# Mixer A of an fp32-split network: TensorE's instructions kept in the order of the text, side work two steps later in the local group, and short chains a step ahead of their transposes

## The chip, the core and the metric

The kernel runs on one core of a Trainium2 chip, whose engines are TensorE (PE in the views, with its weight loads as PEld), VectorE (DVE), ScalarE (ACT), GpSimd (POOL) and SyncE (SP, which issues most transfers). The metric is the device time of one execution in microseconds (us).

## What is computed

A network on 512 tokens of width 1024. Its first half-layer, mixer A, is a dilated attention with three head groups per head: group 0 is local, groups 1 and 2 see keys at strides 4 and 16. The three groups' outputs are mixed by a softmax over their log-sum-exps. Behind mixer A come a feed-forward layer, mixer B (latent attention), and further layers, which the change does not touch.

```python
DIL_CONFIGS = ((128, 1), (512, 4), (2048, 16))   # 8 heads of 128
...
    qkv = (h @ w_qkv).reshape(B, S, 3, N_GROUPS, A_HEADS, A_HEAD_DIM)
    outs, lses = [], []
    for g, (window, dil) in enumerate(DIL_CONFIGS):
        q = rope(rms_norm(qkv[:, :, 0, g], q_gain[g]), S)
        k = rope(rms_norm(qkv[:, :, 1, g], k_gain[g]), S)
        v = qkv[:, :, 2, g]
        o, lse = dilated_group(q, k, v, window, dil)
        outs.append(o)
        lses.append(lse)
    wts = jax.nn.softmax(jnp.stack(lses, 0), axis=0)
    o = wts[0][..., None] * outs[0]
    for g in range(1, N_GROUPS):
        o = o + wts[g][..., None] * outs[g]
    return o.reshape(B, S, A_WIDTH).astype(h.dtype) @ w_o
```

## The kernel before

Every fp32 product is made of three matmuls of split operands (a high and a low part, lines L144 to L146 in `mm3`). A weight tile arrives as `w_raw`, ScalarE copies its high part (`w_hi`, L129) and VectorE its low part (`w_lo`, L130).

Mixer A goes through four quarters `qd` of two heads each, and in each quarter through the groups g = 1, 2, 0. The projection of a group is the main work: groups 1 and 2 take 128x256 or 128x512 products of strided tokens four blocks b at a time, followed by `rotate_pair` for each block; group 0 (`project`) takes q, k and v in turn (`wh` 0 to 2) with `rotate` behind q and k. A rotate is a short serial chain over four engines: ScalarE squares (L419, tile `t`), GpSimd takes powers (L200, L201), ScalarE scales k (`yk`, L426), VectorE multiplies by the tables (L434, L435) and adds (L436). Its scratch tile `t2` exists once, so rotates follow one another. The result `t` is transposed by TensorE (`turn`, L443) and copied out by ScalarE (`qT`, `kT`, L445).

The attention of the group before is the side work. It is a generator that gives up control at each `yield`, and it is stepped once at each `yield` of the projection (12 matmuls in g = 0). `attend_strided` has two turns, two softmax steps, two `flip`s (transposes of the probabilities, L556, with a copy `pt`, L558) and two `values` (L567). `attend_local` turns kT, has four softmax steps (scores L535, mask L543, maximum L545, bias L546, exponentials L549), and then the combine chain that mixes the groups: L614 to L616 on VectorE, an exponential on ScalarE (L617), L618 to L623 on VectorE, which gives the weights `ce`. They are transposed on TensorE (L625, below "the transpose of ce"), copied to `crow` (L627), written to memory and read back as `f` (two transfers one after the other). The probabilities of group 0 are weighted with `ce` (L642), flipped and multiplied with v, and `og` is summed (L648, L649) and split into `oh` and `ol` (L162, L163). A third generator, `post`, is `out_pair`: the output projection of the quarter before (8 steps of 6 matmuls). After the last quarter only the attention of its group 0 is left, with `out_pair` of quarter 2 woven in, and then `out_pair` of quarter 3.

In what order each engine executes all this is not the order of the text: a scheduler reorders the instructions of all engines by its own model of their times. One block of code elsewhere (`Ahead`, a small class) calls a list of functions one ahead: it runs the first when it is made, and at each call returns the result that it holds and runs the next function.

Of the kernel before, what the change touches and what calls it, by code (L numbers as in the profile page):

```python
# [9 lines left out]
F32 = mybir.dt.float32  # L10
# [9 lines left out]
S = 512  # L20
# [36 lines left out]
def drain(gen):  # L57
    for _ in gen:
        pass
# [27 lines left out]
class Net:  # L87
# [253 lines left out]
    def mixer_a(self, pool):  # L341
# [126 lines left out]
        def project_strided(qd, g, u, vs):  # L468

            c0 = g * D + qd * 256  # L470
            wt = wide(c0, 3 * D + c0, nc.gpsimd if (qd, g) == (0, 1) else None)
            tab = tables(qd, g)
            u["rq"] = pool.tile([P, 8], F32, name="rq", tag="rq", bufs=3)
            pre = []
            for bp in range(2):
                for banks in both(wt, bp):
                    if banks:
                        pre += [rotate_pair(u, 2 * bp + i, ps, tab) for i, ps in enumerate(banks)]
                    yield
            u["pre"] = lambda wh: lambda b, h: pre[b][:, (2 * wh + h) * P:(2 * wh + h + 1) * P]  # L480
            if g == 1:
                wt = wide(7 * D + qd * 256, 8 * D + qd * 256)
                v12 = pool.tile([P, NB, 512], F32, name="v12", tag="v12", bufs=1)
                for bp in range(2):
                    for banks in both(wt, bp):
                        for i, ps in enumerate(banks or ()):
                            nc.scalar.copy(out=v12[:, 2 * bp + i, :], in_=ps)  # L487
                        yield
                vs[1], vs[2] = v12[:, :, 0:256], v12[:, :, 256:512]
            u["v"] = vs[g]  # L490
# [62 lines left out]
        def flip(pr):  # L553
            t = self.tbank()
            for n in range(4):
                nc.tensor.transpose(t[:, n * P:(n + 1) * P], pr[:, n * P:(n + 1) * P], self.ident)  # L556
            pt = pool.tile([P, 512], F32, name="pt", tag="pt", bufs=2)
            nc.scalar.copy(out=pt, in_=t)  # L558
            return pt
# [12 lines left out]
        def attend_strided(qd, g, u, og):  # L572

            for wh, n in enumerate("qk"):
                turn(u, n + "T", u["pre"](wh))
                yield
            st = pool.tile([P, 2, 2, NB], F32, name="st", tag="st", bufs=3)
            prs = []
            for h in range(2):
                prs.append(softmax(u, g, h, 0, st))  # L580
                yield
            nc.sync.dma_start(out=st_dram[qd, g - 1].rearrange("n (p b) -> p n b", b=NB),
                              in_=st.rearrange("p s h b -> p (s h) b"))
            pts = []
            for h in range(2):
                pts.append(flip(prs[h]))
                yield
            for h in range(2):
                pv = values(u, g, h, [pts[h]])
                o = pool.tile([P, S], F32, name="og", tag="og", bufs=4)  # L590
                nc.scalar.copy(out=o.rearrange("p (m r) -> p r m", r=4), in_=pv.rearrange("p (r m) -> p r m", r=4))
                og[g, h] = o
                yield

        def attend_local(qd, u, og):

            turn(u, "kT", u["pre"](1))
            s = pool.tile([P, 2, 2, 8], F32, name="cs", tag="cs", bufs=1)
            nc.sync.dma_start(out=s.rearrange("p g s n -> p (g s n)"),
                              in_=st_dram[qd].rearrange("g n (b p) -> p (g n b)", p=P))  # L600
            yield
            st = pool.tile([P, 2, 2, NB], F32, name="st", tag="st", bufs=3)
            prs = []
            for h in range(2):
                for s0 in (0, 2):
                    prs.append(softmax(u, 0, h, s0, st))
                    yield

            own = st.rearrange("p s h b -> p s (h b)")
            T = lambda n, name: pool.tile([P, n, 8], F32, name=name, tag=name, bufs=1)  # L610
            lo, e, dn = T(1, "clo"), T(3, "ce"), T(3, "cd")
            tt = nc.vector.tensor_tensor
            tt(out=lo[:, 0], in0=s[:, 0, 0], in1=s[:, 1, 0], op=ALU.min)
            tt(out=lo[:, 0], in0=lo[:, 0], in1=own[:, 0], op=ALU.min)  # L614
            tt(out=e[:, 0:2], in0=lo.to_broadcast([P, 2, 8]), in1=s[:, :, 0], op=ALU.subtract)
            tt(out=e[:, 2], in0=lo[:, 0], in1=own[:, 0], op=ALU.subtract)  # L616
            nc.scalar.activation(out=e, in_=e, func=AF.Exp)  # L617
            tt(out=dn[:, 0:2], in0=e[:, 0:2], in1=s[:, :, 1], op=ALU.mult)  # L618
            tt(out=dn[:, 2], in0=e[:, 2], in1=own[:, 1], op=ALU.mult)
            tt(out=lo[:, 0], in0=dn[:, 0], in1=dn[:, 1], op=ALU.add)  # L620
            tt(out=lo[:, 0], in0=lo[:, 0], in1=dn[:, 2], op=ALU.add)
            nc.vector.reciprocal(out=lo, in_=lo)
            tt(out=e, in0=e, in1=lo.to_broadcast([P, 3, 8]), op=ALU.mult)  # L623
            t = self.tbank()
            nc.tensor.transpose(t[0:16, 0:P], e[:, 0:2].rearrange("p g n -> p (g n)"), self.ident)  # L625
            row = pool.tile([16, P], F32, name="crow", tag="crow", bufs=1)
            nc.scalar.copy(out=row, in_=t[0:16, 0:P])  # L627
            nc.sync.dma_start(out=f_dram[qd].rearrange("n b p -> (n b) p"), in_=row)
            fs = {}
            for h in range(2):  # L630
                for g in (1, 2):
                    f = pool.tile([P, S], F32, name="f", tag="f", bufs=3)
                    nc.sync.dma_start(out=f, in_=f_dram[qd, (g - 1) * 2 + h].rearrange("b p -> (b p)").partition_broadcast(P))
                    fs[g, h] = f
            yield
            for h in range(2):
                pts = []
                for n in range(2):
                    pr = prs[2 * h + n]
                    for i in range(2):  # L640
                        b = 2 * n + i
                        nc.vector.tensor_scalar(out=pr[:, i * 256:(i + 1) * 256], in0=pr[:, i * 256:(i + 1) * 256],  # L642
                                                scalar1=e[:, 2, h * NB + b:h * NB + b + 1], scalar2=None, op0=ALU.mult)
                    pts.append(flip(pr))
                    yield
                pv = values(u, 0, h, pts)
                for g in (1, 2):
                    tt(out=og[g, h], in0=og[g, h], in1=fs[g, h], op=ALU.mult)  # L648
                    tt(out=og[g, h], in0=og[1, h] if g == 2 else pv, in1=og[g, h], op=ALU.add)  # L649
                oh = pool.tile([P, S], F32R, name="oh", tag="oh", bufs=2)  # L650
                ol = pool.tile([P, S], F32R, name="ol", tag="ol", bufs=2)
                self.split(oh, ol, og[2, h])
                u["o", h] = (oh, ol)
                yield

        side, post = iter(()), iter(())
        for qd in range(4):
            og, vs = {}, {}
            for g in (1, 2, 0):
                u = {"qT": [None, None], "kT": [None, None]}  # L660
                for _ in project_strided(qd, g, u, vs) if g else project(qd, u):
                    next(post, None)
                    next(side, None)
                if g == 1 and qd == 0:
                    nc.sync.dma_start(out=masks, in_=a["k_masks"])

                    for t in (self.hTh, self.hTl):
                        nc.scalar.copy(out=t[:, :, S:S + 64], in_=t[:, :, 0:64].bitcast(F32))
                drain(side)
                drain(post)  # L670
                if g:
                    side = attend_strided(qd, g, u, og)
                else:
                    side = attend_local(qd, u, og)
                if g == 1 and qd in (1, 2):
                    post = self.out_pair(wo, qd - 1, last)
                if g == 0 and qd == 3:
                    post = self.out_pair(wo, 2, last)
                if g == 0:
                    last = u  # L680
        for n in range(11):
            next(side)
            if n > 1:
                next(post, None)
        drain(post)
        drain(side)
        drain(self.out_pair(wo, 3, last))

    def out_pair(self, wo, pr, u):
# [863 lines left out]
```

## Time and profile before

| what | value |
|---|---|
| median of 3 runs | 2560.22 us (2559.7 to 2561.13) |
| the profiled execution's own time | 2559.68 us |
| its span, first to last instruction | 2557.9 us |
| TensorE busy | 2439.0 us (95%) in 13988 matmuls |
| VectorE, ScalarE, GpSimd busy | 1664.4, 1177.3, 269.1 us |
| mean granted TensorE clock | 0.983 |

The span is what the trace covers; the profiled execution took 1.8 us more than that, and was half a microsecond faster than the median. Busy is the time in which an engine had an instruction of its own in work. The granted clock is the share of full speed at which TensorE ran: 1.00 is 2.4 GHz and 0.50 is 1.2 GHz. Mixer A reaches from about 10 to 622 us.

### The profile page before, as it was taken

How to read it: one execution, taken by the hardware profiler on the slowest of the kernel's cores; microseconds unless marked ns; L12 is line 12 of the kernel's file. 1: busy time of each engine (PE TensorE's matmuls, PEld its weight loads, DVE VectorE, ACT ScalarE, POOL GpSimd, SP SyncE). 2: the span in 40 equal slices, each digit the busy share in tenths (PEclk: the TensorE clock that was granted, in tenths of full speed). 3: DMA queues.
4: the chain of work that ended last, by engine and by line, in shares of the span. 5: the costliest groups of instructions: out<-in, count | busy, mean ns of one | idle time of the engine just before them, and what ended most of it. 6: DMA issues, size and time to landing. Idle time of an engine off the chain costs nothing.

```text
span 2557.9 us, 36467 instructions
## 1 busy us (share of the span) xinstructions
PE 2439.0 (95%) x13988; PEld 2159.6 (84%) x13988; DVE 1664.4 (65%) x2718; ACT 1177.3 (46%) x2562; POOL 269.1 (11%) x415
## 2 busy tenths in 40 slices
PE   7999999998999999999999999899998998799998
PEld 7999998997888887677888888899987876799997
DVE  4454454547767645787776646877758775877774
ACT  4554545464332324654332334544445774454442
POOL 5311111120000002320000000000012211100001
PEclk9999999999999999899999999999999999899999
DMA  7342333323555422111564432233332121143332
GB/s 235 117 115 86 101 105 112 112 68 102 191 168 159 141 80 94 33 58 34 182 199 150 148 99 91 92 107 99 100 116 87 55 74 50 50 124 99 100 99 83
DMA packets 230415, 275.97 MB, mean 108 GB/s; under 512 B 43120, under 2 KB 172336, under 8 KB 230240
## 3 DMA queue, kind: packets, MB, share of 16 engines
q1 hardware_dynamic: 229280, 270.49, 34.2%
q0 software_dynamic: 960, 3.15, 0.3%
q8 instruction: 110, 1.80, 0.3%
q14 instruction: 65, 0.53, 0.1%
HBM read 268.21 MB, written 5.38 MB: 107 GB/s over the span
## 4 chain that ended last, share of the span: by engine, by line
PE 74%; DVE 8%; issue 6%; ACT 5%; POOL 4%; DMA 2%; SPq 0%; POOLq 0%; DVEq 0%; ACTq 0%
PE ps_mm L144 21%; PE ps_mm L146 20%; PE ps_mm L145 20%; PE ps_at L144 2%; PE ps_at L145 2%; PE ps_at L146 2%; DMA w_raw<-ffn_w_in 1%; PE ps_tr L443 1%; PE ps_at L567 1%; PE ps_at L535 1%; POOL rk L201 1%; DVE w_lo L130 1%; POOL rq L201 1%; ACT w_hi L129 1%; POOL ss L200 1%
## 5 line engine op out<-in xcount | busy, mean ns | idle before, releaser
L130 DVE TENSOR_TENSOR w_lo<-w_raw,w_hi 128x1024 fp32r<-128x1024 f32 (+2 forms) x304 | 367.8, 1217 | 159.2 <-ACT w_hi L129 157.4
L129 ACT CAST w_hi<-w_raw 128x1024 fp32r<-128x1024 f32 (+2 forms) x308 | 317.0, 1040 | 242.8 <-PE ps_mm L146 165.4
L144 PE MATMUL ps_mm<-w_lo,hTh 128*128 128x256 f32 (+3 forms) x1100 | 390.1, 355 | 4.4 <-DVE t L435 3.5
L145 PE MATMUL ps_mm<-w_hi,hTl 128*128 128x256 f32 (+3 forms) x1100 | 373.3, 339 | 0.9 <-DVE hTl L163 0.9
L146 PE MATMUL ps_mm<-w_hi,hTh 128*128 128x256 f32 (+3 forms) x1100 | 371.8, 338 | 0.0
L144 PE MATMUL ps_mm<-hTl,w_hi 128*128 128x256 f32 (+1 forms) x960 | 324.2, 338 | 5.3 <-DVE hTl L163 4.4
L146 PE MATMUL ps_mm<-hTh,w_hi 128*128 128x256 f32 (+1 forms) x960 | 323.7, 337 | 0.0
L145 PE MATMUL ps_mm<-hTh,w_lo 128*128 128x256 f32 (+1 forms) x960 | 323.7, 337 | 0.0
L144 PEld LDWEIGHTS ps_mm<-w_lo,hTh 128*128 128x128 f32 x1100 | 257.5, 234 | 12.3 <-ACT v L487 3.8
L145 PEld LDWEIGHTS ps_mm<-w_hi,hTl 128*128 128x128 f32 x1100 | 258.4, 235 | 5.9 <-DVE hTl L163 1.5
L146 PEld LDWEIGHTS ps_mm<-w_hi,hTh 128*128 128x128 f32 x1100 | 257.2, 234 | 4.2 <-issue 0.6
L308 DVE TENSOR_TENSOR x_sb<-ps_mm,x_sb 128x512 f32<-128x512 f32 x176 | 120.6, 687 | 130.5 <-PE ps_mm L146 129.8
L144 PEld LDWEIGHTS ps_mm<-hTl,w_hi 128*128 128x128 f32 x960 | 182.2, 190 | 26.2 <-DVE hTl L163 5.1
L146 PE MATMUL ps_mm<-w_hi,ah 128*128 128x512 f32 x512 | 199.7, 390 | 0.0
L144 PE MATMUL ps_mm<-w_lo,ah 128*128 128x512 f32 x512 | 199.6, 390 | 0.0
L145 PE MATMUL ps_mm<-w_hi,al 128*128 128x512 f32 x512 | 199.5, 390 | 0.0
L145 PEld LDWEIGHTS ps_mm<-hTh,w_lo 128*128 128x128 f32 x960 | 182.4, 190 | 19.4
L146 PEld LDWEIGHTS ps_mm<-hTh,w_hi 128*128 128x128 f32 x960 | 182.2, 190 | 18.6
L162 ACT CAST w_hi<-w_raw 128x512 fp32r<-128x512 f32 x160 | 92.4, 619 | 119.0 <-PE ps_mm L146 86.5
L145 PE MATMUL ps_mm<-th,w_lo 128*128 128x256 f32 x480 | 135.8, 283 | 5.8 <-ACT zh L162 5.8
L144 PE MATMUL ps_mm<-tl,w_hi 128*128 128x256 f32 x480 | 137.1, 286 | 1.1 <-DVE pu L1046 0.6
L146 PE MATMUL ps_mm<-w_hi,gh 128*128 128x512 f32 x352 | 137.5, 390 | 0.0
(404 smaller groups left out, 5260.1 us busy)
## 6 DMA issues: line engine op xcount, KB each, us to landing
w_raw<-ffn_w SPq DMA_DIRECT2D x128, 512.0 KB
w_raw<-ffn_w_in SPq DMA_DIRECT2D x88, 512.0 KB
ada_w<-w_ada SPq DMA_DIRECT2D x72, 512.0 KB
w_raw<-a_w_qkv SPq DMA_DIRECT2D x96, 256.0 KB
w_raw<-ffn_w_out SPq DMA_DIRECT2D x44, 512.0 KB
w_raw<-a_w_qkv SPq DMA_DIRECT2D x24, 512.0 KB
w_raw<-w_mix_in SPq DMA_DIRECT2D x20, 512.0 KB
tab<-tab_a SPq DMA_DIRECT2D x36, 256.0 KB
```

The lines of the kernel that those rows point to most:

```text
L129: nc.scalar.copy(out=hi[:, :sz], in_=raw[:, :sz])
L130: (eng or nc.vector).tensor_tensor(out=lo[:, :sz], in0=raw[:, :sz], in1=hi[:, :sz].bitcast(F32), op=ALU.subtract)
L144: mm(ps, lh, rl, start=start, stop=False, skip_group_check=open_)
L145: mm(ps, ll, rh, start=False, stop=False, skip_group_check=open_)
L146: mm(ps, lh, rh, start=False, stop=stop, skip_group_check=open_)
L162: self.nc.scalar.copy(out=hi, in_=src)
L200: self.nc.gpsimd.tensor_scalar(out=ms, in0=ms, scalar1=eps, scalar2=None, op0=ALU.add)
L201: self.nc.gpsimd.tensor_tensor(out=out, in0=ms, in1=self.mhalf[:, :n], op=ALU.pow)
L308: self.nc.vector.tensor_tensor(out=xs, in0=ps, in1=xs, op=ALU.add)
L443: nc.tensor.transpose(t[:, b * P:(b + 1) * P], pick(b, h), self.ident)
L535: nc.tensor.matmul(sc[:, i * kpb * P:(i + 1) * kpb * P], lhs, kT[:, k0:k0 + kpb * P], start=True, stop=True)
L567: nc.tensor.matmul(pv[:, b * P:(b + 1) * P], u["v"][:, (b if g else (b - 1 + i) % NB), h * P:(h + 1) * P], pts[n // 4][:, (n % 4) * P:(n % ...
```

## The change

It has five parts, all in mixer A; no arithmetic is added, removed or resized.

- The whole loop over the quarters stands inside `manual_schedule(engines={PE})`: TensorE's instructions stay in the order of the text. The other engines' order is still the scheduler's.
- In the projection of group 0, the side work (attention of group 2) starts two yields later.
- A `yield` stands between the combine chain and the transpose of `ce` (L636 after).
- The weighting (L642, now `weigh`, L630) is called through `Ahead`, one step ahead of its flip.
- In the tail, `post` is stepped only beside six of the side steps, no longer from the third on beside each.

```diff
             tt(out=e, in0=e, in1=lo.to_broadcast([P, 3, 8]), op=ALU.mult)
+
+            def weigh(h, n):
+
+                pr = prs[2 * h + n]
+                for i in range(2):
+                    b = 2 * n + i
+                    nc.vector.tensor_scalar(out=pr[:, i * 256:(i + 1) * 256], in0=pr[:, i * 256:(i + 1) * 256],
+                                            scalar1=e[:, 2, h * NB + b:h * NB + b + 1], scalar2=None, op0=ALU.mult)
+                return pr
+
+            yield
             t = self.tbank()
             nc.tensor.transpose(t[0:16, 0:P], e[:, 0:2].rearrange("p g n -> p (g n)"), self.ident)
...
+            ahead = Ahead([lambda h=h, n=n: weigh(h, n) for h in range(2) for n in range(2)])
             yield
...
-                    pts.append(flip(pr))
+                    pts.append(flip(ahead()))
                     yield
...
+        with self.tc.manual_schedule(engines={mybir.EngineType.PE}):
+            side, post = iter(()), iter(())
+            for qd in range(4):
...
+                    for n, _ in enumerate(project_strided(qd, g, u, vs) if g else project(qd, u)):
+                        next(post, None)
+
+                        if g or n > 1:
+                            next(side, None)
...
+            for n, _ in enumerate(side):
+                if n in (0, 2, 4, 6, 8, 10):
                     next(post, None)
...
-        for n in range(11):
-            next(side)
-            if n > 1:
-                next(post, None)
-        drain(post)
-        drain(side)
+            drain(post)
         drain(self.out_pair(wo, 3, last))
```

First place: TensorE in quarter 0, at the start of the projection of group 0 (main products `ps_mm<-w_lo,hTh` and the like), where the rotated q of group 2 is turned. The four tiles `t_...` are the rotated blocks b = 0 to 3; each is transposed once for either head. Before, behind the first 24 products:

```order
L146 MATMUL ps_mm<-w_hi,hTh 128x256
L443 MATMUL ps_tr<-ident,t_716 128x128
L443 MATMUL ps_tr<-ident,t_736 128x128
L443 MATMUL ps_tr<-ident,t_842 128x128
L443 MATMUL ps_tr<-ident,t_716 128x128
L443 MATMUL ps_tr<-ident,t_736 128x128
L443 MATMUL ps_tr<-ident,t_842 128x128
L144 MATMUL ps_mm<-w_lo,hTh 128x256
```

After, behind the first 48 products:

```order
L146 MATMUL ps_mm<-w_hi,hTh 128x256
L443 MATMUL ps_tr<-ident,t_718 128x128
L443 MATMUL ps_tr<-ident,t_738 128x128
L443 MATMUL ps_tr<-ident,t_844 128x128
L443 MATMUL ps_tr<-ident,t_864 128x128
L443 MATMUL ps_tr<-ident,t_718 128x128
```

Before, six transposes of three blocks stand together, and the two of the fourth (t_862) follow 31 products later; after, all eight stand together, and the fourth block (t_864) is the fourth instruction of them. The other three quarters are alike, with 17 products in place of 31 before in quarter 1.

Second place: TensorE in quarter 0, during the projection of group 1 of the next quarter, between the last scores of the local attention (`L535`) and its flips (`L556`). Before, 39 products of 128x512 stand between the scores and these rows:

```order
L146 MATMUL ps_mm<-w_hi,hTh 128x512
L625 MATMUL ps_tr<-ident,ce 16x128
L144 MATMUL ps_mm<-w_lo,hTh 128x512
L556 MATMUL ps_tr<-ident,pr 128x128 x4
L145 MATMUL ps_mm<-w_hi,hTl 128x512
L146 MATMUL ps_mm<-w_hi,hTh 128x512
```

After, 24 products stand between the scores and the transpose of `ce`, and 12 more between that and the flips, of which the last is in these rows:

```order
L146 MATMUL ps_mm<-w_hi,hTh 128x512
L636 MATMUL ps_tr<-ident,ce 16x128
L144 MATMUL ps_mm<-w_lo,hTh 128x512
L145 MATMUL ps_mm<-w_hi,hTl 128x512
L146 MATMUL ps_mm<-w_hi,hTh 128x512
```

The transpose of `ce` has moved 15 products towards the scores, and the first flips have moved from one product behind it to 12. Quarters 1 and 2 are alike, also with 39 before and 24 after.

Third place: VectorE in quarter 0, from the maximum of the last softmax step to the weights `ce`. Here `t_1552` and `t_1553` are tiles of a rotate of the projection that goes on beside it. Before:

```order
L545 TENSOR_REDUCE mx<-pr 128x2
L434 TENSOR_TENSOR t_1552<-ps_mm,tab 128x256
L435 TENSOR_TENSOR t_1553<-ps_mm,tab 128x256
L434 TENSOR_TENSOR t_1552<-yk,tab 128x256
L435 TENSOR_TENSOR t_1553<-yk,tab 128x256
L546 TENSOR_TENSOR st<-mx,rq 128x2
L130 TENSOR_TENSOR w_lo<-w_raw,w_hi 128x1024
L436 TENSOR_TENSOR t_1552<-t_1552,t_1553 128x512
L614 TENSOR_TENSOR clo<-clo,st 128x8
```

After:

```order
L545 TENSOR_REDUCE mx<-pr 128x2
L434 TENSOR_TENSOR t_1554<-ps_mm,tab 128x256
L435 TENSOR_TENSOR t_1555<-ps_mm,tab 128x256
L434 TENSOR_TENSOR t_1554<-yk,tab 128x256
L435 TENSOR_TENSOR t_1555<-yk,tab 128x256
L546 TENSOR_TENSOR st<-mx,rq 128x2
L130 TENSOR_TENSOR w_lo<-w_raw,w_hi 128x1024
L436 TENSOR_TENSOR t_1554<-t_1554,t_1555 128x512
L614 TENSOR_TENSOR clo<-clo,st 128x8
```

Nothing has moved here: the bias L546 still stands behind the four multiplications of a rotate, and so on to L623 (a second `w_lo` stands between L616 and L618 in both). Behind L623, the eight weightings stand in one run after, where before a rotate stood between the second and the third.

## Rows read from the trace of the kernel before

**Rows 1.** The page's chain of work that ended last, shares by engine.

```profile
PE 74%; DVE 8%; issue 6%; ACT 5%; POOL 4%; DMA 2%; SPq 0%; POOLq 0%; DVEq 0%; ACTq 0%
```

**Rows 2.** Waits of TensorE, 0 to 640 us: total, times, longest.

```profile
PE ps_tr L443 <- DVE t L436: 16.7, 5, 4.4
...
PE ps_tr L625 <- DVE ce L623: 4.9, 3, 1.6
...
PE ps_tr L556 <- DVE pr L642: 3.0, 4, 0.9
PE ps_mm L144 <- ACT oh L162: 2.9, 1, 2.9
```

**Rows 3.** Timeline of TensorE, quarter 0, transpose of ce: start, duration, [idle before].

```profile
167.72 0.60 PE L144 MATMUL ps_mm<-w_lo,hTh 128*128 128x512 f32 x1
...
178.86 0.28 PE L625 MATMUL ps_tr<-ident,ce 128*16 128x128 f32 x1 [1.62 <-DVE ce L623]
```

**Rows 4.** Timeline of VectorE, quarter 0, the combine chain.

```profile
170.10 0.68 DVE L545 TENSOR_REDUCE mx<-pr 128x2 f32<-128x512 f32 x1
172.86 0.43 DVE L434 TENSOR_TENSOR t<-ps_mm,tab 128x256 f32<-128x256 f32 x1 [2.08 <-ACT yk L426]
...
174.20 0.15 DVE L546 TENSOR_TENSOR st<-mx,rq 128x2 f32<-128x2 f32 x1
...
176.64 1.22 DVE L130 TENSOR_TENSOR w_lo<-w_raw,w_hi 128x1024 fp32r<-128x1024 f32 x1
...
178.62 0.18 DVE L623 TENSOR_TENSOR ce<-ce,clo 128x24 f32<-128x24 f32 x1
```

**Rows 5.** Windows of TensorE: length, busy (matmuls), granted clock, DMA share, GB/s.

```profile
176.00:184.00 8.00, 5.51 (x30) 1.00 0.45 134
...
261.00:264.50 3.50, 3.50 (x20) 0.51 0.89 286
...
538.50:546.50 8.00, 6.15 (x50) 1.00 0.43 132
```

**Rows 6.** Timeline of TensorE, quarter 0, start of group 0 and turn of q.

```profile
100.90 0.36 PE L144 MATMUL ps_mm<-w_lo,hTh 128*128 128x256 f32 x1
...
103.80 0.38 PE L443 MATMUL ps_tr<-ident,t 128*128 128x128 f32 x2
108.61 1.11 PE L443 MATMUL ps_tr<-ident,t 128*128 128x128 f32 x4 [4.43 <-DVE t L436]
```

**Rows 7.** Timelines of VectorE: last rotate of group 2, quarters 0, 1 and 3.

```profile
113.61 0.69 DVE L436 TENSOR_TENSOR t<-t,t 128x512 f32<-128x512 f32 x1
...
258.99 0.69 DVE L436 TENSOR_TENSOR t<-t,t 128x512 f32<-128x512 f32 x1
...
543.88 0.69 DVE L436 TENSOR_TENSOR t<-t,t 128x512 f32<-128x512 f32 x1
```

**Rows 8.** Timelines of TensorE, the same place, quarters 1 and 3.

```profile
250.07 0.36 PE L144 MATMUL ps_mm<-w_lo,hTh 128*128 128x256 f32 x1
...
259.73 0.44 PE L443 MATMUL ps_tr<-ident,t 128*128 128x128 f32 x2 [3.95 <-DVE t L436]
...
533.04 0.36 PE L144 MATMUL ps_mm<-w_lo,hTh 128*128 128x256 f32 x1
...
538.58 0.66 PE L443 MATMUL ps_tr<-ident,t 128*128 128x128 f32 x4 [2.26 <-DVE t L436]
...
544.63 0.44 PE L443 MATMUL ps_tr<-ident,t 128*128 128x128 f32 x2 [1.77 <-DVE t L436]
```

**Rows 9.** Timeline of the tail on VectorE: weights ready, second transfer landed.

```profile
594.41 0.18 DVE L623 TENSOR_TENSOR ce<-ce,clo 128x24 f32<-128x24 f32 x1
...
600.77 0.69 DVE L648 TENSOR_TENSOR og<-og,f 128x512 f32<-128x512 f32 x1 [2.22 <-DMA f<-f_a]
```

**Rows 10.** Timeline of the tail on TensorE: last out_pair, first product behind mixer A.

```profile
604.77 1.23 PE L144 MATMUL ps_mm<-w_lo,oh 128*128 128x512 f32 x4 [2.95 <-ACT oh L162]
...
622.69 0.46 PE L144 MATMUL ps_mm<-hTl,w_hi 128*128 128x256 f32 x1 [1.66 <-DVE hTl L163]
```

More of the change, by code (lines that the diff above doesn't have):

```diff
@@ L638, in attend_local @@
                 for n in range(2):
[L639 to L643, printed above, removed]
-                    pts.append(flip(pr))
+                    pts.append(flip(ahead()))
                     yield
@@ L654, in attend_local @@
                 yield
[L656 to L661, printed above, removed]
-                    next(post, None)
[L663 to L668, printed above, removed]
-                drain(side)
-                drain(post)
[L671 to L680, printed above, removed]
@@ L681, in mixer_a @@
-        for n in range(11):
-            next(side)
-            if n > 1:
-                next(post, None)
-        drain(post)
-        drain(side)
+        with self.tc.manual_schedule(engines={mybir.EngineType.PE}):
+            side, post = iter(()), iter(())
+            for qd in range(4):
+                og, vs = {}, {}
+                for g in (1, 2, 0):
+                    u = {"qT": [None, None], "kT": [None, None]}
+                    for n, _ in enumerate(project_strided(qd, g, u, vs) if g else project(qd, u)):
+                        next(post, None)
+                        if g or n > 1:
+                            next(side, None)
+                    if g == 1 and qd == 0:
+                        nc.sync.dma_start(out=masks, in_=a["k_masks"])
+                        for t in (self.hTh, self.hTl):
+                            nc.scalar.copy(out=t[:, :, S:S + 64], in_=t[:, :, 0:64].bitcast(F32))
+                    drain(side)
+                    drain(post)
+                    if g:
+                        side = attend_strided(qd, g, u, og)
+                    else:
+                        side = attend_local(qd, u, og)
+                    if g == 1 and qd in (1, 2):
+                        post = self.out_pair(wo, qd - 1, last)
+                    if g == 0 and qd == 3:
+                        post = self.out_pair(wo, 2, last)
+                    if g == 0:
+                        last = u
+            for n, _ in enumerate(side):
+                if n in (0, 2, 4, 6, 8, 10):
+                    next(post, None)
+            drain(post)
```

## The prediction, made before the changed kernel ran

> **What bounds the kernel now.** I read the chain of work that ended last first: TensorE holds 74% of it [rows 1], so a change of order pays through TensorE's waits or through its clock. Second, the list of what TensorE waits for inside mixer A [rows 2]: 16.7 us in five waits for the last sum L436 of a rotate ahead of a transpose L443, 4.9 us in three for the weights `ce`, 3.0 us in four for a weighted `pr`, 2.9 us for `oh` in the tail. With smaller ones this is what the change can win; it cannot shorten the products. Third, timelines around these waits [rows 3, 4, 6 to 10]: the reader is to see how many products TensorE has between the instruction that starts a short chain and the transpose that needs its end, and how long that chain takes on the other engines. Fourth, the granted clock [rows 5]: after the 3.95 us wait of quarter 1 it stood at 0.51 for 3.5 us (half speed, 1.2 GHz) with TensorE busy throughout, while it stayed at 1.00 through the 1.62 us wait for `ce` and through quarter 3's pair of 2.26 and 1.77 us with products between. So a long wait is paid twice: the wait, and 3.5 x 0.49 = 1.7 us of lost speed behind it.
>
> **The transpose of ce, quarters 0 to 2.** Before, 39 products separate the last scores from it. They begin at 167.72 and TensorE stands idle from 178.86 - 1.62 = 177.24 [rows 3], so one takes 9.52 / 39 = 0.244 us. `ce` is ready at 178.62 + 0.18 = 178.80 [rows 4], 11.1 us behind the scores. What fills these 11.1 us is not the chain's arithmetic: the maximum is done at 170.78, yet the bias L546 runs at 174.20, because four multiplications of a rotate stand ahead of it on VectorE, and they idled 2.08 us for `yk`; later `w_lo` of 1.22 us stands inside the chain [rows 4]. The change fixes TensorE's order alone; in VectorE's order I find the same rows in the same sequence from the maximum to L623. So I keep 11.1 us. After, 24 products cover 24 x 0.244 = 5.9 us of it, and TensorE stands at the transpose from 173.6 to 178.8: 5.2 us, against 1.62 and the 0.9 for the first weighted tile [rows 2, 3], which 12 products then hide. That is 5.2 - 2.5 = +2.7 us each, **+8.1** for three. Bounds: 0 if the chain shrinks as the cover does, 11.1 - 5.9 = 5.2 each if the wait for the weighted tile comes back elsewhere.
>
> A wait of 5.2 us lies above the one of 3.95 that lost the clock, and far above the 1.62 that did not. I charge one stretch, 1.7 us each: **+5.1** (bounds 0, and two stretches, 10.2).
>
> The Trainium skill, page "PSUM — Partial Sum Buffer", section "Engine vs sequencer instructions", calls the queues of ScalarE, VectorE and GpSimd strictly first in, first out, and says that matmuls start and complete in program order. This speaks against the change: an early place in TensorE's order moves no chain on the other engines forward. The trace agrees where it can: L546 stood behind the rotate for 3.4 us after its maximum was done.
>
> **The turn of q in group 0, four quarters.** It needs the rotated blocks b = 0 to 3 of group 2. Before, three blocks are transposed behind 24 products and the fourth behind 17 or 31 more; after, all behind 48, in the order b0, b1, b2, b3. A 128x256 product takes (103.80 - 100.90) / 24 = 0.121 us [rows 6], so 48 take 5.8 us. The rotates are serial and do not depend on these products, so their ends stay: 113.61 + 0.69 = 114.30, 259.68 and 544.57 in quarters 0, 1 and 3 [rows 7].
> - Quarter 0: TensorE is there at 106.7, waits for b2 to 108.6 (as the row of 4.43 us shows) and for b3 to 114.30. From there five transposes, 14 products and eight transposes of k remain which before were done at about 117.4; at 0.12 to 0.13 us each that is 3.4 us at full speed and 5.1 with one slow stretch, to 119.4: +2.0.
> - Quarter 1: 250.07 + 5.8 and three transposes give 256.3, so a wait of 3.4 us in place of 3.95 [rows 8]: -0.55, the clock falling as before. Quarter 2 has the same pattern: -0.55.
> - Quarter 3: 533.04 + 6.2 = 539.2, a wait of 5.3 in place of 2.26 + 1.77 [rows 8]: +1.3, and a slow stretch that it did not have, 1.7: +3.0.
>
> Sum **+3.9**; bounds -3 (the clock falls nowhere new, quarter 0 even) and +6 (two stretches in quarters 0 and 3).
>
> **The tail.** Before, 48 products of `out_pair` precede the transpose of `ce`; after, 18 do, and 30 follow. `ce` is ready at 594.59 [rows 9]. It comes about 1 us earlier after, since one `w_lo` and some additions leave its chain, but TensorE is there with 30 x 0.244 = 7.3 us less cover, and waits some 7 us. In exchange those 30 products lie under the round trip of `f` (6.2 us from `ce` to L648 [rows 9]) and the wait of 2.95 us for `oh` [rows 10] goes. The end is set by the chain from `ce` through `f`, `oh` and the last `out_pair` rather than by TensorE's idle sum; VectorE's order puts the first `ol` behind the second head's sums, which takes back the 1 us. I take **+0.7** (bounds -2, the chain's whole gain kept with the small waits, and +4, TensorE's 7 less the 2.95).
>
> **At nothing.** The two-yield delay moves group 2's scores, flips and values behind 48 products; VectorE and ScalarE have them done under the 24 products between steps. The early weighting is hidden by the 12 products behind the transpose; without them it costs the 0.9 us seen now. The place of TensorE's other transposes moves by at most 12 products of 0.244 us, 2.9 us.
>
> Sum: 8.1 + 5.1 + 3.9 + 0.7 = +17.8 on the profiled execution's 2559.7 us (0.5 below the median): **2577.5 us**. Without any fall of the clock beyond those seen now, two stretches fewer in the turns (3.4), it would be 8.1 + 3.9 - 3.4 + 0.7 = +9.3, 2569 us.
>
> The Trainium skill, page "TensorE: Matmul & The Clock Gate", section "Why this matters for your kernels", asks for dense matmuls because gaps between bursts bring the clock back to half. By that rule the new waits pay the slow stretch, as in the sum; the case's rows show such a fall behind 3.95 us and none behind 1.62.
>
> **Rivals.**
> - *Faster: the chain fits under 24 products.* If the scheduler's placement under TensorE's new order lets L546 run when its maximum is done (3.4 us earlier) and moves both `w_lo` out (2.3 us), `ce` is ready 5.4 us behind the scores, and the waits of 4.9 and most of 3.0 go: 2559.7 - 7.5 = 2552 us, less if quarter 1's and 2's turns gain too. It decides at 5.9 us. VectorE's listed order speaks against it. 0.08.
> - *No change: waits only change place.* The clock does not fall behind the new waits, the turns come out at their lower bound, and the tail gains 2: 8.1 - 3 - 2 = +3, 2563 us. For it: every chain that TensorE waits for is as long as before. Against it: 3 x 15 products less cover is more than the turns and the tail return. 0.14.
> - *More slower: a queue behind a waiting head.* A rotate's L434 stands behind the weightings on VectorE, and its bank is filled only behind the transpose of `ce`; the next `w_lo` stands behind that rotate, and TensorE's products behind `w_lo`. If that `w_lo` comes late, each of three places costs up to a rotate's idle, 2.08 us [rows 4], or the clock falls for two stretches: +6 or more, 2584 us. The list of waits shows none for a `w_lo` now [rows 2], so there is some slack, and I hold it less likely. 0.18.
>
> **How the numbers follow.** My forecast has 0.60, for 2570 to 2581; the no-change case 0.14, the faster one 0.08, the heavier one 0.18. A range from 2563 to 2586 leaves out the faster case, half of the no-change case and a few hundredths above. A measurement of this kernel tells 0.2% (5.1 us) from no change: slower 0.78, same 0.13, faster 0.09.
>
> **What would show it.** Right: three waits of about 5 us for `ce` at the transpose (now L636), none at the flips behind it; the clock at half behind them; one wait for the fourth rotate in each quarter's turn, largest in quarter 0; a wait near 7 us ahead of the tail's transpose and none for `oh`. Wrong: if the `ce` waits stay under 2 us, the scheduler has taken foreign work out of the chain; if they are there and the total is small, the clock did not fall; if products L144 wait for `w_lo`, the third rival is at work.

## The result, and the profile after

The changed kernel took 2574.84 us (median of 4 runs, 2574.06 to 2576.0) against 2560.68 us before: a ratio of 1.0056, 95% interval 1.0044 to 1.0068. It is slower by some 14 us, and the forecast of 2577.5 us was 2.7 us too high. The span of the profiled execution grew from 2557.9 to 2572.3 us, and the mean granted clock fell from 0.983 to 0.979.

What TensorE waits for, 0 to 660 us of the changed kernel (total, times, longest), answers to [rows 2]:

```profile
PE ps_tr L636 <- DVE ce L623: 20.2, 4, 5.1
PE ps_tr L443 <- DVE t L436: 19.2, 5, 5.4
...
PE ps_mm L144 <- DVE t L435: 2.2, 1, 2.2
PE ps_tr L556 <- ACT pr L549: 0.3, 2, 0.2
```

The wait for `ce` has grown from 4.9 us in three to 20.2 us in four, the turns from 16.7 to 19.2 us; the weighted tiles and `oh` are gone from the list. The third line above, TensorE's first wait for a rotate near 60 us, was longer in the kernel before:

```profile
PE ps_mm L144 <- DVE t L435: 3.5, 1, 3.5
```

The timeline of TensorE has the places of [rows 3, 6 and 8]:

```profile
100.22 0.36 PE L144 MATMUL ps_mm<-w_lo,hTh 128*128 128x256 f32 x1
...
107.93 0.33 PE L443 MATMUL ps_tr<-ident,t 128*128 128x128 f32 x1 [1.65 <-DVE t L436]
113.68 1.33 PE L443 MATMUL ps_tr<-ident,t 128*128 128x128 f32 x5 [5.42 <-DVE t L436]
...
169.16 0.60 PE L144 MATMUL ps_mm<-w_lo,hTh 128*128 128x512 f32 x1
...
180.30 0.38 PE L636 MATMUL ps_tr<-ident,ce 128*16 128x128 f32 x1 [5.13 <-DVE ce L623]
...
255.09 0.36 PE L144 MATMUL ps_mm<-w_lo,hTh 128*128 128x256 f32 x1
...
264.75 1.17 PE L443 MATMUL ps_tr<-ident,t 128*128 128x128 f32 x5 [3.49 <-DVE t L436]
...
330.85 0.38 PE L636 MATMUL ps_tr<-ident,ce 128*16 128x128 f32 x1 [5.09 <-DVE ce L623]
...
557.50 1.33 PE L443 MATMUL ps_tr<-ident,t 128*128 128x128 f32 x5 [5.20 <-DVE t L436]
...
607.94 0.38 PE L636 MATMUL ps_tr<-ident,ce 128*16 128x128 f32 x1 [4.88 <-DVE ce L623]
```

VectorE's timeline in quarter 0 shows that the chain did not get shorter (to compare with [rows 4]):

```profile
171.54 0.68 DVE L545 TENSOR_REDUCE mx<-pr 128x2 f32<-128x512 f32 x1
174.30 0.42 DVE L434 TENSOR_TENSOR t<-ps_mm,tab 128x256 f32<-128x256 f32 x1 [2.08 <-ACT yk L426]
...
175.64 0.16 DVE L546 TENSOR_TENSOR st<-mx,rq 128x2 f32<-128x2 f32 x1
...
178.08 1.23 DVE L130 TENSOR_TENSOR w_lo<-w_raw,w_hi 128x1024 fp32r<-128x1024 f32 x1
...
180.06 0.18 DVE L623 TENSOR_TENSOR ce<-ce,clo 128x24 f32<-128x24 f32 x1
```

The first product behind the scores begins at 169.16 and `ce` is ready at 180.24: 11.1 us, as before, with the same 2.08 us of idle for `yk` in it. And the clock, in windows of TensorE (length, busy, granted clock, DMA share, GB/s), stands at half (0.50) behind each of the long waits shown here, the three for `ce` and the one at the turn of quarter 3:

```profile
180.00:183.00 3.00, 2.70 (x7) 0.50 0.57 186
331.00:336.00 5.00, 5.00 (x13) 0.50 0.49 159
484.00:486.00 2.00, 2.00 (x6) 0.50 0.74 246
557.00:561.00 4.00, 3.50 (x17) 0.50 0.35 123
```

**Where the time went.** I cut mixer A at two marks in each quarter: the first product of group 0, and the first product behind the last local scores. From the first to the second mark lies the turn, from the second mark to the first of the next quarter lies the transpose of `ce`. Quarter 0's marks before are 100.90 and 167.72 us and quarter 1's first is 250.07 [rows 6, 3, 8]; after they are 100.22, 169.16 and 255.09. All four quarters, from the same rows of the two timelines:

| stretch | before, us | after, us | difference | of which waits | forecast |
|---|---|---|---|---|---|
| start to 100.90 | 100.90 | 100.22 | -0.7 | -1.3 | 0 |
| turns, quarters 0 to 3 | 66.82, 65.19, 65.45, 52.95 | 68.94, 64.64, 65.50, 55.19 | +2.1, -0.55, +0.05, +2.2 | +2.6, -0.5, -0.8, +1.2 | +2.0, -0.55, -0.55, +3.0 |
| `ce`, quarters 0 to 2 | 82.35, 82.35, 69.98 | 85.93, 87.24, 73.65 | +3.6, +4.9, +3.7 | +2.6 each | +4.4 each |
| last scores (585.99, 601.31) to the end | 1971.9 | 1971.0 | -0.9 | | +0.7 |

They add up to +14.4 us, the growth of the span: 12.1 us at the transpose of `ce`, 3.9 at the turns, and -0.7 and -0.9 at the start and behind the last scores. These last two are not shown to be more than chance, since the table compares one execution of each kernel: d4, d4y48, y36 and y48 below, whose text is the changed kernel's up to the first mark, reach it at 100.83, 101.54, 99.10 and 98.96 us; and from the last scores to the end d4 and sh1, with the same tail, take 1971.9 and 1970.6 us.

### The profile page after: what moved, and what is told of

Its sections match the earlier page's. It is cut to its first block, busy times and chain, and to the rows that moved or that the text cites. A ratio compares the mean times of both kernels' runs of the same rounds, so it can differ in the third digit from the quotient of the medians.

```text
span 2572.3 us, 36473 instructions
## 1 busy us (share of the span) xinstructions
PE 2443.5 (95%) x13988; PEld 2162.6 (84%) x13988; DVE 1664.7 (65%) x2718; ACT 1177.5 (46%) x2562; POOL 269.2 (10%) x415
## 4 chain that ended last, share of the span: by engine, by line
PE 75%; DVE 8%; issue 6%; ACT 5%; POOL 4%; DMA 2%; SPq 0%; POOLq 0%; ACTq 0%; DVEq 0%
PE ps_mm L144 21%; PE ps_mm L146 20%; PE ps_mm L145 20%; PE ps_at L144 2%; PE ps_at L145 2%; PE ps_at L146 2%; DVE w_lo L130 1%; PE ps_at L567 1%; PE ps_tr L443 1%; ACT w_hi L129 1%; DMA w_raw<-ffn_w_in 1%; POOL rk L201 1%; PE ps_tr L851 1%; PE ps_tr L145 1%; PE ps_tr L144 1%
## 5 line engine op out<-in xcount | busy, mean ns | idle before, releaser
L145 PE MATMUL ps_mm<-w_hi,gl 128*128 128x512 f32 x352 | 137.9, 392 | 0.0
```

Source lines behind the costliest of these rows:

```text
L145: mm(ps, ll, rh, start=False, stop=False, skip_group_check=open_)
```

## The experiments

Each kernel differs from the changed one as its diff says (manual_only: from the kernel before); nothing is left out of the computation in any. The kernel before ran beside them, at 2560.9 to 2561.0 us.

**y36 and y48: more products ahead of the transpose of ce**

```diff
             yield
+            yield          # y36: one more, y48: two more
             t = self.tbank()
             nc.tensor.transpose(t[0:16, 0:P], e[:, 0:2].rearrange("p g n -> p (g n)"), self.ident)
```

> The changed kernel with one more yield between the combine chain and the transpose of ce: 36 products in place of 24 lie between the last scores and the transpose. Theory (the loss is the cover taken from a chain whose length VectorE's order sets): the waits of 5.1 us in quarters 0 to 2 shrink by 12 x 0.244 = 2.9 to about 2.2 us each, and the clock no longer falls behind them, as it did not behind 2.26 us in the kernel before: about -13 us, 2562. If the clock falls behind 2.2 us too, -9 us, 2566. Rival (the chain moves along with its place in the text, or the loss is elsewhere): waits of 5 us stay, 2575.

> The changed kernel with two more yields there: 48 products, 11.7 us of cover for a chain of 11.1 us. Theory: the waits for ce in quarters 0 to 2 go to nothing, and the clock stays up behind them: the three places cost 12 us more than before the change, and held 2.5 us of waits each before it, so about -19 us, 2555. The step from 36 to 48 products is then worth 3 x 2.2 = 6.6 us. Rival: no gain over the changed kernel, 2575, or a new wait where the flips and values now come 24 products later.

Measured: y36 2559.3 us, ratio to the kernel before 0.999 (0.9981 to 1.0); y48 2553.38 us, 0.9968 (0.9955 to 0.998). Timeline and windows of TensorE in y36:

```profile
178.63 0.28 PE L637 MATMUL ps_tr<-ident,ce 128*16 128x128 f32 x1 [2.24 <-DVE ce L623]
```

```profile
174.00:186.00 12.00, 9.76 (x45) 1.00 0.45 124
320.00:332.00 12.00, 9.70 (x43) 1.00 0.38 115
467.00:479.00 12.00, 9.78 (x44) 1.00 0.38 117
```

The waits are 2.24, 2.30 and 2.22 us, 2.9 less than 5.1, and the clock stays at 1.00 through them. In y48's list of waits, 100 to 560 us, `ce` is gone:

```profile
PE ps_tr L443 <- DVE t L436: 19.0, 5, 5.4
PE ps_tr L556 <- ACT pr L549: 0.4, 2, 0.2
```

The rivals fell: the waits did not stay, and no new one came up at the flips. With VectorE's chain at an unchanged 11.1 us (`ce` ready at 178.58 in y48, the scores' mark at 167.52), the cover decides the wait. y48 also measures what a stretch of `ce` costs with neither wait nor slow clock. Its marks in quarter 0, and a window over the place, are these:

```profile
167.52 0.60 PE L144 MATMUL ps_mm<-w_lo,hTh 128*128 128x512 f32 x1
...
247.11 0.36 PE L144 MATMUL ps_mm<-w_lo,hTh 128*128 128x256 f32 x1
```

```profile
165.00:185.00 20.00, 20.00 (x88) 1.00 0.32 90
```

That is 79.6 us; in quarters 1 and 2 it takes 79.6 and 67.1. The changed kernel's 85.93, 87.24 and 73.65 lie 6.3, 7.6 and 6.6 us above, 20.6 of the 21.5 us by which y48 is faster than it. Of each, 5.1 is the wait, which leaves 1.2, 2.6 and 1.5 us for the slow clock, 5.2 in all by the unrounded differences. The products' own pace in the changed kernel bears this out: behind the three waits 6, 12 and 7 products of 128x512 start 0.43 us apart, in place of 0.24.

**d4 and d4y48: the turn of q behind 96 products**

```diff
-                        if g or n > 1:
+                        if g or n > 3:
                             next(side, None)
```

d4y48 has this and y48's two yields.

> The changed kernel with the side work of group 0's projection two yields later still, so that q of group 2 is turned behind 96 products, not 48. Theory (the rotates end when they end; TensorE only has to come later): the waits at this turn, 7.1, 3.5, 3.5 and 5.2 us, all go, with four slow stretches of some 1.7 us: about -26 us, 2549. Rival (delayed side work is late for its own successors: scores, flips and values of group 2, and the local attention behind them): the waits move to later places, and the time stays within 5 us of 2575.

> Both: q of group 2 turned behind 96 products, and 48 products ahead of the transpose of ce. Theory: the two gains add, -19 - 26, about 2530 us, below the kernel before. Rival: a common limit (an engine that feeds both places) lets through only the larger of the two, about 2549.

Measured, both far from the theory: d4 2578.42 us, 1.0062 (1.0047 to 1.0077), no gain over the changed kernel; d4y48 2560.38 us, 0.9994 (0.9985 to 1.0003): with y48's yields the delay costs 7 us against y48 alone. The waits of d4's TensorE, 120 to 640 us:

```profile
PE ps_tr L636 <- DVE ce L623: 20.3, 4, 5.1
PE ps_tr L556 <- ACT qT L445: 20.1, 4, 5.1
```

Between 20 and 660 us 1.65 us of the 19.2 for L436 is left, so the rotates had indeed ended in time. But 20.1 us have come back at the flips of group 2's probabilities, which wait for ScalarE's copy `qT`. ScalarE's timeline in quarter 0 has the place:

```profile
133.35 0.49 ACT L549 ACTIVATE pr<-pr,st,rq 128x128 f32<-128x128 f32 x1
...
134.83 0.59 ACT L445 COPY qT<-ps_tr 128x512 f32<-128x512 f32 x1
136.42 1.14 ACT L400 ACTIVATE yk<-ps_mm,rk 128x128 f32<-128x128 f32 x4 [1.00 <-POOL rk L201]
137.43 0.60 ACT L445 COPY qT<-ps_tr 128x512 f32<-128x512 f32 x1
```

With the later side work the turn of group 0's own q (eight transposes from 129.34) comes between group 2's scores and its flips. It fills both banks for transposes, and the copies that free them stand on ScalarE behind group 2's exponentials and a rotate: the first flip starts at 135.47, just when the first copy is done. The rival was right that the waits move to a later place, but not by lateness of the side work: a bank was held.

**d4y48t: d4y48 with that turn moved out of the way**

```diff
-                    if wh == 1 and bp == 1:
+                    if wh == 2 and bp == 1:
                         turn(u, "qT", pick(0))
```

> The run with 96 and 48 products, and the turn of group 0's own q moved from behind its k to behind its v, so that the two transpose banks are free when group 2's flips come. Theory (in that run TensorE waited 5.0 to 5.1 us in each quarter at the first flip, for a bank that ScalarE's copies of qT release behind eight exponentials): these four waits, 20 us, and the slow clock behind them go, to about 2534 us. Rival (the flips wait for their exponentials anyway, or the late turn waits in its turn): 2555 or more.

Measured: 2532.22 us, 0.9881 (0.9866 to 0.9896). Its list of waits, 100 to 640 us:

```profile
PE ps_tr L638 <- DVE ce L623: 3.0, 1, 3.0
PE ps_tr L250 <- DVE h_nrm L235: 2.8, 4, 1.2
PE ps_tr L443 <- DVE t L436: 1.7, 1, 1.7
PE ps_tr L556 <- ACT pr L549: 1.0, 3, 0.7
```

The four waits of 5 us are gone, and against d4y48 28 us with them; this one line decides whether the longer delay pays.

**nosched and manual_only: the two halves of the change**

```diff
-        with self.tc.manual_schedule(engines={mybir.EngineType.PE}):
+        if True:                                   # nosched: the changed text, not pinned
```

```diff
-        side, post = iter(()), iter(())
-        for qd in range(4):
+        with self.tc.manual_schedule(engines={mybir.EngineType.PE}):   # manual_only: the text of before, pinned
+            side, post = iter(()), iter(())
+            for qd in range(4):
```

> The changed text without the pinning: the scheduler orders TensorE too. It then puts 39 products ahead of the transpose of ce, as before the change, 48 ahead of the turn of q, and 36 ahead of the tail's transpose. Theory (the loss is the cover that the pinned order takes from ce, 12 us, and the turns cost 4 us by themselves): about 2563 us, with 1.6 us waits for ce. Rival (the text's other edits, the delay and the early weighting, cost the time whichever engine orders it): 2570 or more.

> The text of the kernel before with TensorE pinned to it, and nothing else of the change: 12 products stand ahead of the transpose of ce, 24 ahead of the turn of q. Theory: a wait is the chain's length less its cover, so 11.1 - 2.9 = 8.2 us for ce, three times, and at the turns 10.2, 6.5, 6.9 and 8.3 us; with the slow clock behind each some 25 us more than the changed kernel, about 2600. Rival (the chains follow TensorE's order, so that cover does not matter): about the changed kernel's 2575.

Measured: nosched 2558.83 us, 0.9992 (0.9983 to 1.0002); manual_only 2594.66 us, 1.0126 (1.0111 to 1.0141). Waits of nosched, 100 to 600 us, then of manual_only, 20 to 660 us, and timeline rows of manual_only in quarter 0:

```profile
PE ps_tr L443 <- DVE t L436: 17.1, 5, 4.3
PE ps_tr L636 <- DVE ce L623: 5.6, 4, 1.6
```

```profile
PE ps_tr L443 <- DVE t L436: 30.0, 6, 6.3
PE ps_tr L625 <- DVE ce L623: 25.1, 4, 7.0
```

```profile
112.56 1.33 PE L443 MATMUL ps_tr<-ident,t 128*128 128x128 f32 x5 [5.27 <-DVE t L436]
...
181.25 0.38 PE L625 MATMUL ps_tr<-ident,ce 128*16 128x128 f32 x1 [7.00 <-DVE ce L623]
```

The text's edits cost nothing that can be measured when the scheduler orders TensorE; pinning costs 16 us on the new text and 34 on the old. The old puts only 12 products ahead of `ce` and 24 ahead of the turn, and both waits are longer for it: 25.1 us in place of the changed kernel's 20.2, and 30.0 in place of 19.2. The edits thus give back about 20 us of what the pinning takes. The `ce` wait in manual_only was 7.0 us, not 8.2: there the second `w_lo` stands outside the chain, which took 181.19 - 171.06 = 10.1 us.

**sh1: the same cover, another meeting of chain and rotates**

```diff
-                        if g or n > 1:
+                        if n > (1, 0, -1)[g]:
```

> The changed kernel with the side work of group 1 (the local attention) one yield later, so that it meets the rotates of that group at another place; still 24 products between the last scores and the transpose of ce. In VectorE's order only a w_lo then stands between the last maximum and its bias, no rotate. Theory (the chain is long because foreign work stands in it on VectorE): 11.1 us less a rotate's 3.4 us, so the waits of 5.1 us fall to about 2 with the same cover, the clock stays up behind them, and the time falls by 3 x 3 + 5 = 14 us, to about 2561. Rival (the length is the chain's own, or set by TensorE's place alone): waits of 5 us, 2575.

Measured: 2561.29 us, 1.0 (0.9991 to 1.0009), 13.6 us below the changed kernel. VectorE's and TensorE's timelines in quarter 0:

```profile
177.16 0.68 DVE L545 TENSOR_REDUCE mx<-pr 128x2 f32<-128x512 f32 x1
177.75 1.22 DVE L130 TENSOR_TENSOR w_lo<-w_raw,w_hi 128x1024 fp32r<-128x1024 f32 x1
178.89 0.16 DVE L546 TENSOR_TENSOR st<-mx,rq 128x2 f32<-128x2 f32 x1
...
181.43 0.18 DVE L623 TENSOR_TENSOR ce<-ce,clo 128x24 f32<-128x24 f32 x1
```

```profile
181.66 0.38 PE L636 MATMUL ps_tr<-ident,ce 128*16 128x128 f32 x1 [2.52 <-DVE ce L623]
```

The bias now runs 1.7 us after its maximum began, where it took 4.1, and the chain from the scores (173.14) is 8.5 us long. The waits are 2.52, 2.48 and 2.53 us with 24 products, where y36 had 2.24 with 36: taking a rotate out of the chain is worth nearly as much as 12 more products of cover. So the rival fell here too: the length of 11.1 us is not the chain's own.

**y48tail and d4y48t_tail: y48 and d4y48t with another order in the tail**

```diff
-                if n in (0, 2, 4, 6, 8, 10):
+                if n in (4, 5, 6, 7, 8, 10, 11, 13):
                     next(post, None)
```

> The run with 48 products ahead of the transpose of ce, and in the tail all scores first, then 24 products of out_pair ahead of the transpose of ce, in place of 12 between the scores and 12 behind. Theory (the tail's end is set by the chain from the scores through ce, f and oh, not by TensorE's idle sum): the scores come 12 x 0.244 = 2.9 us earlier, the wait of 4.7 us for ce shrinks below 3, and the time falls by 1 to 3 us. Rival (TensorE's idle sum counts): by up to 4.7 us. A third way: VectorE's four softmax steps are the chain, and nothing changes.

> The fastest run so far (96 and 48 products, the late turn) with the tail of the other run: all scores first, then 24 products ahead of the transpose of ce. That tail was worth 2.5 us there. Theory: the same here, 2529 to 2530 us. Rival: here the tail's scores stand right behind two turns and wait for their copies, and the gain is below 1 us.

Measured: y48tail 2550.85 us, 0.9956 (0.9941 to 0.9971), d4y48t_tail 2529.38 us, 0.9882 (0.9867 to 0.9897). The tail's wait for `ce` fell from 4.66 to 1.31 us in y48tail, a 1.12 us wait of the scores for VectorE came up, and the medians are 2.5 and 2.8 us lower than without it. But the ratios' intervals overlap (in the second pair the ratios are equal), so that gain stays unproven, and with it which chain sets the tail's end. d4y48t, with or without it, is 1.2% faster than the kernel before and some 1.7% faster than the changed one.

## Why the prediction was right

The forecast was slower, +17.8 us on the profiled execution; the measured growth was 14.4 us of span. The mechanism was the one forecast: cover taken from chains whose length VectorE's order sets, and a slow clock behind the new waits. By its own steps:

- **The transpose of ce.** Wait forecast 5.2 us, found 5.13, 5.09, 5.09. That VectorE's order keeps the chain at 11.1 us held to 0.1 us, and sh1 showed its reason: take the rotate out of the chain and it is 8.5 us. Fall of the clock forecast 5.1 us in sum, found 5.2 (from y48's undisturbed stretches). That it fell at all three was right; that the sum agrees is partly luck, since 1.7 us each was forecast and 1.2, 2.6 and 1.5 came out. The whole term was 13.2 in the forecast and 12.1 found: the kernel before also lost a little at these places outside the two waits that I counted, 0.3 us each (82.35 - 79.6 - 2.5). The upper bound of 5.2 us each left out the 1.62 already paid before; by its own condition it is 3.6.
- **The turns.** +3.9 forecast, +3.9 found, but the equal sums are luck: quarter 2 came out 0.6 us worse than forecast and quarter 3 0.8 better. Waits in quarters 0, 1 and 3 forecast as two pieces of 1.9 and 5.6, 3.4, and 5.3 us; found 1.65 and 5.42, 3.49, 5.20. In quarter 2 the wait fell from 4.25 to 3.48 us, but half speed behind it lasted longer (products 0.21 us apart until 421.8, some 5 us, where before it ended after 3.4 us) and took the gain back. In quarter 3 the clock took 1.1 us rather than 1.7. The bounds given for this term were off: with no new fall of the clock and quarter 0 even, the forecast's own waits give -0.55 - 0.55 + 1.3 = +0.2, not -3, and two more stretches on +3.9 give +7.3, not +6. The no-change rival, which took the -3, should have stood near 2566 us.
- **The tail.** Mis-sized: "TensorE ... waits some 7 us", found 4.88, and +0.7 became -0.9. The 7 is the whole lost cover of 7.3 us, without even the 1 us taken off by which the chain was expected to come earlier; from the last scores to `ce` it shrank by 2 us (601.31 to 607.88 us in place of 585.99 to 594.59). That the end came out 0.9 us ahead is no more than d4 and sh1 differ there with the same tail, so only this is shown: no loss clear of chance came of the longer wait.
- **At nothing.** The start, which the forecast left out, came out 0.7 us shorter, with TensorE's first wait for a rotate, near 60 us, at 2.22 us in place of 3.50. I had not looked there; but this wait is 1.88 us in y48 and 3.67 in d4y48, whose text is the same up to there, so the gain is not shown to come from the change. No wait came up in the changed kernel that could be put down to the two-yield delay, but it has little room: two more yields cost 20 us of bank waits (d4).
- **The rivals.** That L546 might run when its maximum is done did not happen, and the third rival's late `w_lo` did not either: no product waits for one in mixer A. The no-change rival's "clock does not fall" is refuted by the windows.

The Trainium skill, page "PSUM — Partial Sum Buffer", section "Engine vs sequencer instructions", says that VectorE's queue is strictly first in, first out. The trace after agrees: with its maximum done at 172.22 the bias still ran at 175.64, behind the rotate; in y36 and y48, where TensorE's order has the transpose 12 and 24 products later, it ran just as late, 3.4 us behind its maximum.

## What to carry to other kernels

In these runs a short chain over other engines took a time that VectorE's order set (11.1 us, 10.1 in manual_only, 8.5 in sh1), wherever TensorE's order put its end; what TensorE waited was that time less the products placed between the chain's start and the transpose that ends it. Before pinning an order by hand, count these products for each chain, take the chain's time from the trace with all foreign work that stands in it, and give it that much cover (or take the foreign work out): here 24, 36 and 48 products ahead of a chain of 11.1 us gave waits of 5.1, 2.2 and 0 us. Then look at what the shifted work meets: a transpose that holds a PSUM bank until a copy comes through a busy ScalarE cost about as much (20.1 us) as the waits that the shift had removed (17.5 us).

## What was not expected of the hardware

The slow stretch behind a wait is not a function of the wait's length alone. Three waits of 5.09 to 5.13 us cost 1.2, 2.6 and 1.5 us more than themselves, and d4's three of 5.11 us at the same places 1.3, 1.6 and 1.7; behind quarter 1's the clock stood at 0.50 from 331 to 336 us at least, about twice as long as behind quarter 0's, where the products were back at their full pace at 183.05. In sh1 the wait of 2.52 us in quarter 0 was followed by a slow stretch, and those of 2.48 and 2.53 us in quarters 1 and 2 by none, as the windows show (length, busy, granted clock, DMA share, GB/s):

```profile
178.00:182.00 4.00, 1.49 (x7) 0.88 0.43 130
182.00:186.00 4.00, 4.00 (x15) 0.69 0.49 136
326.00:330.00 4.00, 1.52 (x8) 1.00 0.43 132
330.00:334.00 4.00, 4.00 (x20) 1.00 0.44 132
476.00:480.00 4.00, 3.74 (x18) 1.00 0.60 185
```

In the changed kernel the wait of only 2.22 us near 59 us was followed by half speed as well (products 0.43 us apart, windows at 0.77 and 0.80), while y36's three of 2.2 to 2.3 us were not. What else decides was not tried.
